# First stage of a decoder layer: x loaded by chunks, weight tiles contiguous, constants multiplied before x is there, seven PSUM banks, token rows loaded into the output buffer

## The chip, the cores and the metric

The kernel runs on one core of one Trainium2 chip. The metric is the device time of one execution in microseconds (us), the median of several runs. Beside it stands one profiled execution, from which every trace number comes. TensorE is called PE in the profile, its weight load PEld, VectorE DVE, ScalarE ACT, GpSimd POOL and SyncE SP; SP issues nearly all DMAs, in order.

## What is computed

One inference step of one decoder layer for 1024 prompt tokens and 8 x 4 sample tokens (1056 in all), model width 1024, in float32: a mixer (chunked gated MLP beside latent attention), cross-attention into a memory, and a gated convolution FFN. The change is in the first stage, the input projection:

```python
u, v, cq, ckv, kpe = split_in(rms_norm(xp, g_mix[l]) @ w_in[l])
a_out, _ = chunk_gmlp(u, v, w_s[l], b_s[l], ln_v_g[l], ln_v_b[l])
```

`chunk_gmlp` takes gelu(v), a layer norm over each group of 64 channels, multiplies each chunk of 128 tokens by a causal 128 x 128 matrix per group, adds a bias and multiplies by gelu(u). The same is done for the sample tokens.

## The kernel before, in words

**Split products.** A float32 operand is split into a high part (rounded to `FR`, float32r) and the rest, by `split` (L187): ScalarE makes the high part (L191, or L195 with the gain g_mix as scale), VectorE the low part (L192, L198). A product is three matmuls, high x high, high x low, low x high (`mm3`, L185).

**Order.** The framework orders the instructions of each engine when the kernel is built, by the order in which they are written and by its own simulated time; once built, the order of each engine is fixed. Between L337 and L428 a manual schedule keeps SP's DMAs in the written order.

**x twice.** The projection needs x with the 1024 channels on the partitions (input `xT`, 8 slices k of 128 channels), in three chunks of 384, 384 and 288 tokens (`CH`). Each chunk is loaded in two halves of four slices into `xr` (L317) and split into `xh`, `xl` (L353). The scale of rms_norm, one number per token, is applied after the projection; it needs x with tokens on the partitions (input `x`, nine token tiles `TILES` of 128, the last of 32). `squares` (L324) sums the squares of a tile on ScalarE (L332) and takes the inverse root on VectorE by a chain of eleven small instructions (`rsqrt`, L210 to L236); the result stands in `rs_tok`. Token tiles 0 to 2 go to buffers `xt` beside `xr` (L343 to L347). The pool of `xt` and `xr` is closed before `a_all`, the buffer of the stage's output, is opened in the same place (L365 to L367), and token tiles 3 to 8 are loaded into `a_all` while it is still unused (L371, L426).

**Weights.** The projection's columns come in six pieces: v0, v1, u0, u1 (256 columns each, u1 with the 32 of kpe) and a0, a1. `wraw` loads one in two halves into a buffer of [128, 8, 288], two such buffers in turn; of the 288 columns only the first n are used, so one row of a DMA is n elements. `wsplit` splits it.

**The loop** (L411) runs over two halves `hf`. In each, `proj` (L358) makes the v product of a token tile, 24 matmuls of 256 columns, into one of five PSUM banks with the tag "mm" (three more have the tag "st"); gelu with the scale rs_tok empties the bank on ScalarE (L435). Layer norm follows by groups of tiles (0 to 2, 3 to 5, 6 and 7, 8) on VectorE (L436 to L446), and on GpSimd with the gain and bias that `rows` brings (L448, L450, L453). After the first group of the first half, `gate_matrices` (L379) loads w_s, makes it causal on GpSimd (L383), splits it and prepares the sample tokens' version. Then come the nine u products (L464, gelu into `a_all` at L465), and the products of the gate matrices with the normed v (L474, L480). The rest of the stage makes the latents from a0 and a1 (L516 on). Later stages read `xT` once more as the residual (`out_proj`).

Of the kernel before, what the change touches and what calls it, by code (L numbers as in the profile page):

```python
# [5 lines left out]
F32 = mybir.dt.float32  # L6
FR = mybir.dt.float32r
I32 = mybir.dt.int32
AF = mybir.ActivationFunctionType
# [4 lines left out]
P = 128  # L14
NP_, NS, NT = 1024, 32, 1056
# [6 lines left out]
CH = [(0, 384), (384, 384), (768, 288)]  # L22
# [132 lines left out]
class Net:  # L155
# [132 lines left out]
    def phase1(self):  # L288
        nc, tc, I, O = self.nc, self.tc, self.I, self.O
        p = self.open("p1")  # L290
# [3 lines left out]
        pr = self.open("p1r", side="right")  # L294
        raws = {}

        def wraw(name, src, n):
            raws[name] = raw = self.t(pr, [P, 8, 288], F32, "wraw", 2)[:, :, :n]
# [13 lines left out]
        xts, xrs = [], []  # L312

        def xload(c, e):
            o, n = CH[c]
            xrs.append(self.t(px, [P, 4, 384], F32, "xr", 6)[:, :, :n])
            nc.sync.dma_start(xrs[-1], I["xT"][:, 4 * e : 4 * e + 4, o : o + n])  # L317

        def tload(i, place):
            t0, tn = TILES[i]  # L320
            xts.append(place[:tn])
            nc.sync.dma_start(xts[-1], I["x"][t0 : t0 + tn])

        def squares(p, i0, i1):  # L324

            ss = self.t(p, [P, 4], F32, "ss", 2)[:, : i1 - i0]
            if i1 == 9:
                nc.vector.memset(ss, 1.0)
            for i in range(i0, i1):
                xt = xts[i]  # L330
                tn = xt.shape[0]
                nc.scalar.activation(xt, xt, AF.Square, accum_out=ss[:tn, i - i0 : i - i0 + 1])  # L332
            self.rsqrt(p, self.rs_tok[:, i0:i1], ss, 1.0 / 1024)

        xt = lambda: self.t(px, [P, 1024], F32, "xt", 3)
        loads = tc.manual_schedule(engines={mybir.EngineType.SP})
        loads.__enter__()  # L337
        raws["v0"] = raw = self.t(pr, [P, 8, 288], F32, "wraw", 2)[:, :, :256]
# [4 lines left out]
        tload(0, xt())  # L343
        for e in range(2):
            xload(1, e)
        tload(1, xt())
        tload(2, xt())  # L347
        for e in range(2):
            xload(2, e)
# [8 lines left out]
        def proj(w, i, n):  # L358
            t0, tn = TILES[i]
            ps = self.t(pp, [P, 512], F32, "mm", 5)[:tn, :n]  # L360
# [5 lines left out]
        pl = self.open("pl")  # L366
        a_all = self.t(pl, [P, 9, 512], F32, "a_all")  # L367

        flat = a_all.rearrange("p i n -> p (i n)")
        for i in range(3, 7):  # L370
            tload(i, flat[:, (i - 3) * 1024 : (i - 2) * 1024])  # L371
# [4 lines left out]
        lng, lnb = rows[:, :512], rows[:, 512:]  # L376
        gates = {}

        def gate_matrices():  # L379

            ws = self.t(pg, [P, 8, P], F32, "ws")
            nc.sync.dma_start(ws, I["w_s"])
            nc.gpsimd.affine_select(ws, ws, [[0, 8], [1, P]], ALU.is_ge, 0.0, base=0, channel_multiplier=-1)  # L383
# [3 lines left out]
            sel = self.t(pg, [P, NS], F32, "sel")  # L387
            nc.sync.dma_start(sel, I["c_sel"])
            blk = self.t(pg, [NS, NS], F32, "blk")
            nc.sync.dma_start(blk, I["c_blk"])  # L390
            wsc = self.t(pg, [P, 8, ND], F32, "wsc")
            nc.gpsimd.tensor_copy(wsc, ws[:, :, :ND])
            st = self.t(pp, [P, 512], F32, "st", 3)
            nc.tensor.matmul(st[:NS, :32], sel, wsc.rearrange("p g t -> p (g t)"), start=True, stop=True)
# [12 lines left out]


        wraw("v1", I["w_v1"], 256)
        nc.sync.dma_start(self.ident, I["c_ident"])  # L410
        for hf in range(2):  # L411
            c0 = hf * 256
            nu = 288 if hf else 256
# [5 lines left out]
            vgs = self.t(pg, [NS, 256], F32, "vgs")  # L419
            for i0, i1 in ((0, 3), (3, 6), (6, 8), (8, 9)):  # L420
                m, tn = i1 - i0, TILES[i0][1]
                if hf == 0 and i0 in (3, 6):
                    squares(pg, i0, i0 + 3)
                if hf == 0 and i0 == 3:
                    for i in range(7, 9):
                        tload(i, flat[:, (i - 7) * 1024 : (i - 6) * 1024])  # L426
                    wraw("u1", I["w_u1"], 288)
                    loads.__exit__(None, None, None)  # L428
                gv = self.t(pg, [P, 3, 4, 64], F32, "gv", 2)[:tn, :m]
                mu = self.t(pg, [P, 3, 4], F32, "mu", 2)[:tn, :m]  # L430
                rv = self.t(pg, [P, 3, 4], F32, "rv", 2)[:tn, :m]
                for i in range(i0, i1):
                    ps = proj(w, i, 256)
                    g, mi = gv[:, i - i0], mu[:, i - i0]
                    nc.scalar.activation(g.rearrange("p g d -> p (g d)"), ps, AF.Gelu_apprx_tanh, scale=self.rs_tok[:tn, i : i + 1])  # L435
                    nc.vector.tensor_reduce(mi, g, AX.X, ALU.add)  # L436
                    nc.vector.tensor_scalar(mi, mi, 1.0 / 64, None, ALU.mult)
                    nc.vector.tensor_tensor(g, g, mi.unsqueeze(2).broadcast_to([tn, 4, 64]), ALU.subtract)
                    sq = self.t(pg, [P, 4, 64], F32, "gsq", 2)[:tn]
                    nc.scalar.activation(sq, g, AF.Square)  # L440
                    nc.vector.tensor_reduce(rv[:, i - i0], sq, AX.X, ALU.add)
                rf = rv.rearrange("p m g -> p (m g)")
                self.rsqrt(pg, rf, rf, 1.0 / 64)
                for i in range(i0, i1):
# [7 lines left out]
                    else:  # L452
                        nc.gpsimd.tensor_tensor(vgs, gf, lnb[:tn, c0 : c0 + 256], ALU.add)  # L453
                        nc.sync.dma_start(O["o_vg"][:, c0 : c0 + 256], vgs)
                if hf == 0 and i0 == 0:
                    gate_matrices()
                    wsh, wsl, bs_s, wss = (gates[x] for x in ("wsh", "wsl", "bs_s", "wss"))
            if hf == 0:
                w = wsplit("v1")
                wraw("a0", I["w_a"][0], 256)  # L460
            else:
                w = wsplit("a0")
            for i, (t0, tn) in enumerate(TILES):
                ps = proj(wu, i, nu)  # L464
                nc.scalar.activation(a_all[:tn, i, c0 : c0 + 256], ps[:, :256], AF.Gelu_apprx_tanh, scale=self.rs_tok[:tn, i : i + 1])  # L465
# [1101 lines left out]
    def out_proj(self, pp, p, mxs, ws, xh, xl, r3, end):  # L1567
# [741 lines left out]
```

## Time and profile before

| | us |
|---|---|
| median of 3 runs (lowest, highest) | 1870.41 (1868.35, 1872.27) |
| the profiled execution's own time | 1873.17 |
| its span, first to last instruction | 1871.5 |
| TensorE busy in the span | 1812.4 |
| VectorE, ScalarE, GpSimd busy | 1382.2, 928.9, 708.0 |
| mean granted TensorE clock | 0.991 |

A row of the order in time reads: start, duration, engine, line, operation, out<-in, shape, count, and in brackets the engine's idle time before it and what ended that. A wait row reads: who waited for whom, us in total, times, longest. A busy TensorE is not one at its peak, since matmuls overlap.

### The profile page before, as it was taken

The numbers are of one execution on the slowest core, as the hardware profiler recorded it, in microseconds if no ns is written. First come the engines' busy times: TensorE is split into PE (matmuls) and PEld (weight loads), VectorE is DVE, ScalarE is ACT, GpSimd is POOL, SyncE is SP. The second block draws the span as 40 slices with busy tenths as digits, with TensorE's granted clock in tenths as the row PEclk, the third lists the DMA queues.
The fourth block names the chain that finished last, engine by engine and source line by source line (L and its number), as shares of the span: only waits on it lengthen the run. The fifth ranks groups of instructions, "written<-read, shape, count | busy, mean of one in ns | idle before, by whom it ended". The sixth has DMA issues, their size and how long they took to land.

```text
span 1871.5 us, 39806 instructions
## 1 busy us (share of the span) xinstructions
PE 1812.4 (97%) x14402; PEld 1746.4 (93%) x14402; DVE 1382.2 (74%) x2883; ACT 928.9 (50%) x1965; POOL 708.0 (38%) x826
## 2 busy tenths in 40 slices
PE   6999899989999999999999999999999999999999
PEld 6999799889999999998799988899999999999999
DVE  6865967766887667776744676888888888878664
ACT  6435676666555655555533455633333333344442
POOL 1221515643535454443313110267776677500000
PEclk9999899999999999999999999999999999999999
DMA  8202204666776667564554345422222222495242
GB/s 286 70 10 68 82 1 165 222 230 175 219 205 186 180 173 200 162 186 128 182 157 134 135 158 154 129 67 81 81 82 90 69 72 77 113 352 167 78 154 76
DMA packets 139784, 260.18 MB, mean 139 GB/s; under 512 B 20546, under 2 KB 82851, under 8 KB 136515
## 3 DMA queue, kind: packets, MB, share of 16 engines
q1 hardware_dynamic: 138722, 256.58, 43.8%
q8 instruction: 114, 1.87, 0.4%
q10 hardware_dynamic: 864, 1.05, 0.2%
q14 instruction: 84, 0.68, 0.1%
HBM read 212.27 MB, written 45.30 MB: 138 GB/s over the span
## 4 chain that ended last, share of the span: by engine, by line
PE 61%; issue 5%; SPq 3%; DMA 3%; DVE 3%; POOL 2%; ACT 1%; POOLq 0%; DVEq 0%; ACTq 0%
PE d L185 12%; PE s L185 11%; PE b L185 7%; PE F L185 7%; PE X L185 6%; PE E L185 6%; PE A L185 3%; PE y L185 3%; DMA cT<-cT 2%; SPq L1220 2%; SPq L1224 1%; PE o L1367 1%; PE t L185 1%; POOL cl L1252 1%; PE v L185 1%
## 5 line engine op out<-in xcount | busy, mean ns | idle before, releaser
L185 PE MATMUL s<-w2h,ch 128*128 128x288 f32 (+1 forms) x1024 | 303.7, 297 | 0.0
L185 PE MATMUL s<-w2h,cl 128*128 128x288 f32 (+1 forms) x1024 | 296.0, 289 | 4.2 <-POOL cl L1252 3.0
L185 PE MATMUL s<-w2l,ch 128*128 128x288 f32 (+1 forms) x1024 | 294.6, 288 | 0.0
L185 PEld LDWEIGHTS s<-w2h,ch 128*128 128x128 f32 x1024 | 192.6, 188 | 8.3 <-ACT sq L1292 2.5
L185 PEld LDWEIGHTS s<-w2h,cl 128*128 128x128 f32 x1024 | 192.4, 188 | 6.5 <-POOL cl L1252 5.0
L185 PEld LDWEIGHTS s<-w2l,ch 128*128 128x128 f32 x1024 | 192.8, 188 | 0.0
L1295 DVE TENSOR_REDUCE ss<-sq 128x16 f32<-128x1024 f32 x128 | 155.3, 1213 | 32.4 <-ACT sq L1292 32.2
L1252 POOL TENSOR_TENSOR cl<-cT,ch 128x512 fp32r<-128x512 f32 x64 | 83.7, 1307 | 113.2 <-ACT ch L1248 92.5
L1292 ACT ACTIVATE sq<-s 128x512 f32<-128x512 f32 x128 | 76.6, 598 | 88.8 <-PE s L185 88.7
L1289 ACT ACTIVATE sq<-s 128x512 f32<-128x512 f32 x128 | 76.7, 600 | 74.5 <-PE s L185 74.0
L191 ACT CAST a<-brb 128x528 fp32r<-128x528 f32 x77 | 48.8, 634 | 111.4 <-PE d L185 107.9
L185 PE MATMUL mm<-whi,xh 128*128 128x256 f32 (+3 forms) x288 | 83.4, 291 | 16.4 <-ACT xh L195 10.0
L192 DVE TENSOR_TENSOR a<-brb,a 128x528 fp32r<-128x528 f32 x77 | 54.3, 707 | 58.3 <-ACT a L191 58.3
L185 PE MATMUL d<-a,w 128*128 128x264 f32 x768 | 95.4, 284 | 0.5 <-DVE G L2087 0.5
L185 PEld LDWEIGHTS d<-a,w 128*128 128x128 f32 x768 | 94.3, 188 | 0.7 <-issue 0.7
L932 PEld LDWEIGHTS o<-v,pth 128*128 128x128 f32 x576 | 75.7, 197 | 8.4 <-ACT pth L922 4.2
L185 PE MATMUL mm<-wlo,xh 128*128 128x256 f32 (+3 forms) x288 | 82.1, 288 | 0.0
L185 PE MATMUL mm<-whi,xl 128*128 128x256 f32 (+3 forms) x288 | 82.1, 289 | 0.0
L932 PE MATMUL o<-v,pth 128*128 128x64 f32 x576 | 76.3, 274 | 5.6 <-ACT pth L922 3.3
L1958 POOL TENSOR_TENSOR lo<-s,hi 128x1024 fp32r<-128x1024 f32 x20 | 62.9, 3142 | 45.7 <-ACT hi L1957 45.7
L1248 ACT CAST ch<-cT 128x512 fp32r<-128x512 f32 x128 | 73.4, 625 | 3.7 <-DMA cT<-cT 3.6
L2013 ACT COPY a<-A 128x264 f32<-128x264 f32 x43 | 16.1, 375 | 118.7 <-PE A L185 113.9
(725 smaller groups left out, 6447.5 us busy)
## 6 DMA issues: line engine op xcount, KB each, us to landing
cT<-cT SPq DMA_DIRECT2D x256, 160.0 KB, 2.8
ck<-ck SPq DMA_DIRECT2D x256, 144.0 KB, 3.4
raw<-w_up SPq DMA_DIRECT2D x44, 512.0 KB, 3.6
wsumd<-wsum SPq DMA_DIRECT2D x13, 1024.0 KB, 4.2
actd<-cv SPq DMA_DIRECT2D x44, 264.0 KB, 2.4
brb<-actd SPq DMA_DIRECT2D x44, 264.0 KB, 5.6
wsum<-w_down SPq DMA_DIRECT2D x11, 1024.0 KB, 5.0
raw<-wsumd SPq DMA_DIRECT2D x20, 512.0 KB, 3.7
```

Source lines behind the costliest of these rows:

```text
L185: self.nc.tensor.matmul(out, l, r, start=first and i == 0, stop=last and i == len(seq) - 1)
L191: {"act": nc.scalar.copy, "pool": nc.gpsimd.tensor_copy, "dve": nc.vector.tensor_copy}[eng](hi, src)
L192: low = lambda: nc.vector.tensor_tensor(lo, src, hi, ALU.subtract)
L932: nc.tensor.matmul(u["o"][:, e], th[:, z * P : z * P + P], s["v"][:, jj, h % 4], start=j == z == 0, stop=e == 1 and jj == 2 * G + 1)
L1220: dmas.append([nc.sync.dma_start(cT[:, j], I["cT"][bass.ds(rv, 1)].rearrange("a p n -> (a p) n")) for j, rv in enumerate(rvs)])
L1224: nc.sync.dma_start(ck[j * 32 : j * 32 + 32], I["ck"][bass.ds(rv, 1)].rearrange("a t s f -> (a t) s f"))
L1248: nc.scalar.copy(d["h"][:, k], src[k])
L1252: (nc.vector if k else nc.gpsimd).tensor_tensor(d["l"][:, k], src[k], d["h"][:, k], ALU.subtract)
L1289: nc.scalar.activation(sq[:, 0], ps[:, :, n0 : n0 + 256], AF.Square)
L1292: nc.scalar.activation(sq[:, 1], pt.rearrange("p (e d) -> p e d", e=2), AF.Square)
L1295: yield lambda: nc.vector.tensor_reduce(s["ss"][:, g0 : g0 + 2].rearrange("p e (z h) -> p z e h", z=2), sq.rearrange("p z e (h d) -> p z e ...
L1958: eng.tensor_tensor(lo, src, hi, ALU.subtract)
```

## The change

`xT` is stored chunk after chunk, so that a half chunk is one contiguous row of up to 1536 elements per partition, and `xr` has the same shape; a weight tile takes the first 8n elements of its buffer without gaps. `a_all` is opened before `xr`, in a place of its own, and every token tile is loaded into it: tile i takes the quarter i % 4, so tiles 4 to 8 wait until the square of the tile four before is done. `squares` takes three tiles at a time. `busy` multiplies a tile of ones (and then the first arrived pieces of w_v0 and xT) on TensorE into a bank that nobody reads, before the first product of x. The v0 products of the first six tiles are written ahead of the loop, the sixth and the seventh of them in "st" banks, and the remaining ones and two u0 products before the gelus of their groups. The loads of w_s and two small constants go into the manual order behind `rows`, and `gate_matrices` is called after all four groups of the first half instead of after the first.

```diff
-    o["xT"] = f(x.T.reshape(8, P, NT).transpose(1, 0, 2))
+    xT = x.T.reshape(8, P, NT).transpose(1, 0, 2)
+    o["xT"] = f(np.concatenate([xT[:, :, c : c + n].reshape(P, 8 * n) for c, n in CH], 1))
...
+        def wtile(n):
+            return self.t(pr, [P, 8, 288], F32, "wraw", 2).rearrange("p k n -> p (k n)")[:, : 8 * n].rearrange("p (k n) -> p k n", k=8)
...
+        pl = self.open("pl")
+        a_all = self.t(pl, [P, 9, 512], F32, "a_all")
         px = self.open("px")
...
+        st0 = self.t(pp, [P, 512], F32, "st", 3)
+        warm = self.t(px, [P, 512], F32, "warm")
+        nc.vector.memset(warm, 1.0)
+        def busy(x, n):
+            for _ in range(n):
+                nc.tensor.matmul(st0[:, : x.shape[1]], warm[:, :P], x, start=True, stop=True)
...
+        def tload(i):
             t0, tn = TILES[i]
+            xts.append(flat[:tn, i % 4 * 1024 : i % 4 * 1024 + 1024])
+            nc.sync.dma_start(xts[i], I["x"][t0 : t0 + tn])
...
+        busy(warm, 4)
+        raws["v0"] = raw = wtile(256)
         for e in range(2):
             k = slice(4 * e, 4 * e + 4)
             nc.sync.dma_start(raw[:, k], I["w_v0"][:, k])
             xload(0, e)
+            if e == 0:
+                busy(raw[:, :2].rearrange("p k n -> p (k n)"), 1)
+                busy(xrs[0][:, 0, :256], 1)
+        for i in range(3):
+            if i:
+                for e in range(2):
+                    xload(i, e)
+            tload(i)
         w = wsplit("v0")
         for c, (o, n) in enumerate(CH):
             for k in range(8):
                 self.split(xh[:, k, o : o + n], xl[:, k, o : o + n], xrs[2 * c + k // 4][:, k % 4], self.col("g_mix", k))
-            if c == 0:
-                squares(px, 0, 1)
-            elif c == 1:
-                squares(px, 1, 3)
+            if c == 1:
+                squares(0)
...
         self.close("px")
+        for i in range(3, 6):
+            tload(i)
         wraw("u0", I["w_u0"], 256)
+        tload(6)
+        squares(1)
+        for i in range(7, 9):
+            tload(i)
+        wraw("v1", I["w_v1"], 256)
         pg = self.open("pg")
...
+        ready = {i: proj(w, i, 256, ("mm", 5) if i < 5 else ("st", 3)) for i in range(6)}
+        us = {}
...
                 if hf == 0 and i0 == 3:
-                    for i in range(7, 9):
-                        tload(i, flat[:, (i - 7) * 1024 : (i - 6) * 1024])
+                    squares(2)
+                    ready[6] = proj(w, 6, 256, ("st", 3))
+                    ready[7] = proj(w, 7, 256)
                     wraw("u1", I["w_u1"], 288)
                     loads.__exit__(None, None, None)
+                elif hf == 0 and i0 == 6:
+                    ready[8] = proj(w, 8, 256)
+                    for i in range(2):
+                        us[i] = proj(wu, i, 256)
...
-                if hf == 0 and i0 == 0:
-                    gate_matrices()
-                    wsh, wsl, bs_s, wss = (gates[x] for x in ("wsh", "wsl", "bs_s", "wss"))
             if hf == 0:
+                gate_matrices()
+                wsh, wsl, bs_s, wss = (gates[x] for x in ("wsh", "wsl", "bs_s", "wss"))
                 w = wsplit("v1")
...
-            nc.sync.dma_start(res, I["xT"][:, m, o : o + n])
+            nc.sync.dma_start(res, I["xT"][:, 8 * o + m * n : 8 * o + m * n + n])
```

More of the change, by code (lines that the diff above doesn't have):

```diff
@@ L295, in phase1 @@
         raws = {}
+        def wtile(n):
+            return self.t(pr, [P, 8, 288], F32, "wraw", 2).rearrange("p k n -> p (k n)")[:, : 8 * n].rearrange("p (k n) -> p k n", k=8)
         def wraw(name, src, n):
-            raws[name] = raw = self.t(pr, [P, 8, 288], F32, "wraw", 2)[:, :, :n]
+            raws[name] = raw = wtile(n)
             for k in range(0, 8, 4):
@@ L324, in squares @@
-        def squares(p, i0, i1):
-            ss = self.t(p, [P, 4], F32, "ss", 2)[:, : i1 - i0]
-            if i1 == 9:
-                nc.vector.memset(ss, 1.0)
[L329 to L335, printed above, removed]
+            xrs.append(self.t(px, [P, 4, 384], F32, "xr", 6).rearrange("p k n -> p (k n)")[:, : 4 * n].rearrange("p (k n) -> p k n", k=4))
@@ L336, in phase1, with squares @@
+        def squares(c):
+            ss = self.t(pl, [P, 3], F32, "ss", 3)
+            if c == 2:
+                nc.vector.memset(ss, 1.0)
+            for i in range(3):
+                xt = xts[3 * c + i]
+                nc.scalar.activation(xt, xt, AF.Square, accum_out=ss[: xt.shape[0], i : i + 1])
+            self.rsqrt(pl, self.rs_tok[:, 3 * c : 3 * c + 3], ss, 1.0 / 1024)
         loads = tc.manual_schedule(engines={mybir.EngineType.SP})
         loads.__enter__()
-        raws["v0"] = raw = self.t(pr, [P, 8, 288], F32, "wraw", 2)[:, :, :256]
+        busy(warm, 4)
@@ L342, in phase1 @@
             xload(0, e)
[L343 to L349, printed above, removed]
+            if e == 0:
+                busy(raw[:, :2].rearrange("p k n -> p (k n)"), 1)
+                busy(xrs[0][:, 0, :256], 1)
+        for i in range(3):
+            if i:
+                for e in range(2):
+                    xload(i, e)
+            tload(i)
         w = wsplit("v0")
@@ L365, in phase1 @@
         self.close("px")
[L366 to L371, printed above, removed]
-        wraw("u0", I["w_u0"], 256)
+        for i in range(3, 6):
+            tload(i)
+        wraw("u0", I["w_u0"], 256)
+        tload(6)
[3 more added lines that the diff above has]
+        wraw("v1", I["w_v1"], 256)
         pg = self.open("pg")
@@ L376, in phase1 @@
         lng, lnb = rows[:, :512], rows[:, 512:]
+        ws = self.t(pg, [P, 8, P], F32, "ws")
+        nc.sync.dma_start(ws, I["w_s"])
+        sel = self.t(pg, [P, NS], F32, "sel")
+        nc.sync.dma_start(sel, I["c_sel"])
+        blk = self.t(pg, [NS, NS], F32, "blk")
+        nc.sync.dma_start(blk, I["c_blk"])
         gates = {}
         def gate_matrices():
-            ws = self.t(pg, [P, 8, P], F32, "ws")
-            nc.sync.dma_start(ws, I["w_s"])
             nc.gpsimd.affine_select(ws, ws, [[0, 8], [1, P]], ALU.is_ge, 0.0, base=0, channel_multiplier=-1)
```

26 lines of the change are left out of this document (9 added, 17 removed).

## The prediction

> **What bounds the kernel now.** I read the table of engines first, then the waits of the first 72 us, then TensorE (PE) and the engines that feed it in order of time, and last a table by stretches (in its rows, after the stretch: its length; busy us and instructions of PE, PEld, DVE, ACT, POOL; granted clock, DMA share, GB/s).
>
> ```profile
> PE 1812.4 (97%) x14402; PEld 1746.4 (93%) x14402; DVE 1382.2 (74%) x2883; ACT 928.9 (50%) x1965; POOL 708.0 (38%) x826
> ...
> PE mm L185 <- ACT xh L195: 10.0, 1, 10.0
> ...
> PE mm L185 <- ACT gv L435: 6.2, 2, 4.2
> ...
> SPq L322 <- DMA xr<-xT: 11.6, 1, 11.6
> ...
> 57.00:125.00 68.00, 68.00 (x545) 66.73 (x545) 51.23 (x158) 24.11 (x54) 22.07 (x27) 1.00 0.07 20
> ```
>
> TensorE is busy 97% of the span and without a break from 57 to 125 us, so what this stage can win is what TensorE loses before 57. The waits name it: 10.0 us until the first split x, and 6.2 us in two stops that ended when ScalarE's gelu (gv, L435) emptied a PSUM bank. VectorE has 16.8 us free in those 68, so work that it owes there can be paid later. The stops, and two stretches at half clock:
>
> ```profile
> 9.97 0.58 PE L185 MATMUL mm<-whi,xh 128*128 128x256 f32 x1 [9.97 <-ACT xh L195]
> ...
> 12.48 0.41 PE L185 MATMUL mm<-wlo,xh 128*128 128x256 f32 x1
> 12.70 0.33 PE L185 MATMUL mm<-whi,xl 128*128 128x256 f32 x1
> ...
> 12.98 0.28 PE L185 MATMUL mm<-wlo,xh 128*128 128x256 f32 x1
> 13.10 0.28 PE L185 MATMUL mm<-whi,xl 128*128 128x256 f32 x1
> ...
> 27.66 0.39 PE L185 MATMUL mm<-whi,xh 128*128 128x256 f32 x1 [1.96 <-ACT gv L435]
> 40.70 0.42 PE L185 MATMUL mm<-whi,xh 128*32 128x256 f32 x1 [4.21 <-ACT gv L435]
> 51.35 0.38 PE L185 MATMUL mm<-whi,xh 128*128 128x256 f32 x1 [0.29 <-ACT a_all L465]
> ```
>
> Up to 12.70 one matmul starts 0.21 us after the other, then 0.12. So from 9.97 to about 12.8 the array ran at half rate: 2.8 us that full rate does in 1.55, a loss of 1.25. The stop of 4.21 us brought this back, and here the granted clock (the third number from the right) shows it:
>
> ```profile
> 41.00:42.00 1.00, 1.00 (x7) 0.79 (x6) 1.00 (x4) 0.37 (x2) 1.00 (x2) 0.50 1.09 351
> ...
> 43.00:44.00 1.00, 1.00 (x9) 0.84 (x8) 1.00 (x3) 0.34 (x1) 1.00 (x2) 0.74 1.03 384
> ```
>
> From 40.7 to 43.5 again 2.8 us, again 1.25 lost. TensorE's losses before 57 are thus 9.97 + 1.25 + 1.96 + 4.21 + 1.25 + 0.29. Why the banks were late is in the feeding engines (SPq is the DMA queue on SP):
>
> ```profile
> 27.91 1.76 SPq L322 DMA_DIRECT2D a_all<-x  x4
> ...
> 26.00:27.00 1.00, 0.00 (x0) 0.00 (x0) 0.99 (x4) 1.00 (x3) 0.00 (x0) 1.00 0.00 0
> ...
> 25.44 1.81 ACT L195 ACTIVATE xh<-xr,cols 128x288 fp32r<-128x288 f32 x4 [1.17 <-DMA xr<-xT]
> 27.16 0.45 ACT L435 ACTIVATE gv<-mm,rs_tok 128x256 f32<-128x256 f32 x1
> ...
> 35.93 1.06 ACT L332 ACTIVATE a_all<-a_all 128x1024 f32<-128x1024 f32 x1 [0.19 <-DMA a_all<-x]
> 38.58 1.22 DVE L192 TENSOR_TENSOR wlo<-wraw,whi 128x1024 fp32r<-128x1024 f32 x1 [0.16 <-ACT whi L191]
> 38.94 1.04 ACT L191 CAST whi<-wraw 128x1024 fp32r<-128x1024 f32 x1 [0.40 <-DMA wraw<-w_u]
> 40.17 1.21 ACT L435 ACTIVATE gv<-mm,rs_tok 128x256 f32<-128x256 f32 x3 [0.18 <-DVE rs_tok L236]
> ```
>
> Token tiles 3 to 6 of x are issued only at 27.91, because their place overlaps the buffers of xT; the DMAs stand still (0 GB/s at 26:27). So the last square of tiles 3 to 5 starts at 35.93, their scale rs_tok is there at 40.1, and only then can gelu empty banks. The first stop is gelu of tile 0, held in ScalarE's order behind the last piece of xT (25.44).
>
> **The change part by part.**
>
> *Token x into a_all from the start.* This takes the 11.6 us wait out of SP's queue. Ahead of tiles 3 to 5 stand 7.0 MB (cols 0.07, w_v0 1.05, xT 4.33, three token tiles 1.57), which at some 380 GB/s from 3 us (rows of the start, below) end at 21.5; the next 1.57 MB need 4 us and land at about 26, nearly 10 us before 35.9; w_u0 follows at about 29. It adds waits: tiles 4 to 8 reuse places, so their loads, and u0, v1, rows and w_s behind them on SP, wait for squares on ScalarE. The first squares come behind chunk 1's split, about 18 us, before SP's DMAs run dry. I take nothing; a square that comes late holds these loads back, and costs at most the second stop and its cold stretch over again.
>
> *Seven banks.* The first seven tiles of v0 need no gelu; two more tiles are 2 x 24 matmuls x 0.12 = 5.7 us of work, more than the first stop. The scale of tiles 0 to 2 now needs all three token tiles, landing at some 21 to 22; with three squares and one root about 26.5. TensorE, starting at 8.6, has filled seven banks at 8.6 + 7 x 2.86 = 28.6. So 1.96 goes. After nine tiles (34.3) it needs w_u0, landed at 29, split with 2 x 1.04 on ScalarE and 2 x 1.22 on VectorE, and banks of tiles 3 to 5, whose scale I put at 31 to 33. So 4.21, its half clock of 1.25 and the 0.29 go; each release now comes only 1 to 3 us before it is needed, a thin cover that VectorE's load can use up (below).
>
> *The start.* Three terms meet: landing, split, warming.
>
> ```profile
> 6.58 1.04 ACT L191 CAST whi<-wraw 128x1024 fp32r<-128x1024 f32 x1 [4.28 <-DMA wraw<-w_v]
> 9.31 2.13 ACT L195 ACTIVATE xh<-xr,cols 128x384 fp32r<-128x384 f32 x4 [1.68 <-DMA xr<-xT]
> ...
> 3.00:4.00 1.00, 0.00 (x0) 0.00 (x0) 0.00 (x0) 0.00 (x0) 0.00 (x0) 1.00 1.00 210
> 4.00:5.00 1.00, 0.00 (x0) 0.00 (x0) 0.00 (x0) 0.00 (x0) 0.00 (x0) 1.00 0.92 234
> ...
> 6.00:7.00 1.00, 0.00 (x0) 0.00 (x0) 0.00 (x0) 0.42 (x1) 0.00 (x0) 1.00 1.03 364
> 7.00:8.00 1.00, 0.00 (x0) 0.00 (x0) 0.34 (x1) 0.63 (x1) 0.00 (x0) 1.00 1.07 387
> ...
> 31.00:32.00 1.00, 1.00 (x11) 1.00 (x10) 0.00 (x0) 0.28 (x1) 0.00 (x0) 1.00 1.07 426
> ```
>
> At 3:5 the queue carries w_v0 in rows of 1 KB and moves 210 to 234 GB/s with the DMA engines 92 to 100% busy; at 31:32 it carries rows of 4 KB and moves 426. Contiguous tiles make the first rows 4 and 6 KB. At 400 GB/s from 3.0 us the remaining 1.2 MB up to the first half of chunk 0 are through at 6.0, and land 1 to 1.9 later (the slowest engine): 7.0 to 7.9 in place of 9.2. The split adds 0.6: 7.6 to 8.5.
>
> Warming stands before it on TensorE: four products of 512 plain f32 columns, one more on w_v0, one of 256 on x. The trace has none that wide. The nearest rows:
>
> ```profile
> 50.45 0.25 PE L394 MATMUL st<-wsc,sel 128*32 128x32 f32 x2
> 1093.67 0.60 PE L1679 MATMUL t<-ident,pr 128*128 128x128 f32 x4
> ...
> 9.96 2.21 DVE L198 SCALAR_TENSOR_TENSOR xl<-xr,cols,xh 128x384 fp32r<-128x384 f32 x4 [1.07 <-ACT xh L195]
> ```
>
> One call is two instructions (L394), and 128 columns follow each other by (0.60 - 0.27) / 3 = 0.11 us; so 512 columns cost 2 x 0.44 = 0.87 us, 1.75 at half clock. The memset of 512 columns is not in the trace; one on 384 takes 0.55 (xl: four in 2.21), so TensorE can begin at about 1.4. With 2.8 us at half clock, as in both stretches above, the four end at 6.3, the fifth at 7.2, the sixth at 7.6 or when x lands. All at half clock they would end at 1.4 + 7.0 + 1.75 + 0.87 = 11.0. I take the first product at 8.6, near the short end because both measured stretches are short: a gain of 1.4, with ends of +2.4 and -1.0. The warming also covers the cold 1.25, which goes. The Trainium skill ("TensorE: Matmul & The Clock Gate", Part 1) has the gate look at free-running windows of about 3.4 us, so a burst may see almost two before it is freed; the traced 2.8 fits one. By two windows the first product would be near 9.5 and the sum 0.9 smaller.
>
> *The rest.* The gate matrices come later, and one of four root chains on VectorE goes (11 instructions of 0.16 = 1.8 us). Neither is on TensorE's path while VectorE keeps up. Loads of xT in the output stage keep their rows: 0.
>
> **Sum:** 1.4 + 1.25 + 1.96 + 4.21 + 1.25 + 0.29 = 10.4 us. The profiled execution took 1873.17 us (span 1871.5), so 1862.8 of its kind; the median of the runs shown, 1870.41, is 2.8 lower, and the forecast against it is **1860.0**.
>
> **Rivals.**
>
> *The first x lands no earlier.* The low rate at 3:5 can be the queue's start, not its rows: at 6:8 rows of 1 and 1.5 KB run at 364 to 387. Then the first product stays at 9.97, and only 9.0 is won: **1861.4**. The Trainium skill speaks for it: "DMA: Bandwidth & Descriptors" (Specifications) has full rate from 512 B on, so rows of 1 KB would lose nothing; the traced 210 beside 426 speaks against.
>
> *VectorE becomes the bound.*
>
> ```profile
> 7.50:57.00 49.50, 40.57 (x316) 39.17 (x317) 42.38 (x133) 34.75 (x68) 10.21 (x12) 0.97 0.81 285
> 33.21 0.74 DVE L441 TENSOR_REDUCE rv<-gsq 128x4 f32<-128x256 f32 x2 [2.35 <-ACT gsq L440]
> 42.14 1.10 DVE L437 TENSOR_SCALAR mu<-mu 128x4 f32<-128x4 f32 x3
> ```
>
> It has 42.4 us of work between 7.5 and 57, 40.6 without the root chain; with TensorE 10.4 earlier the stretch, from about 6.0 to 46.6, is 40.6 long: full. Idle such as the 2.35 behind ScalarE's gsq, and operations stretched beside GpSimd (three of 0.16 in 1.10), leave no room. For it to cost nothing, what is late must be layer norm, which TensorE needs only after u0, not rs_tok or the low weight parts. If some 5 us of such idle stay in front of these, VectorE is through at 51.6, and 5.4 is won: **1865.0**.
>
> *Gate matrices too late (slower).* They now stand behind all layer norms of the first half on GpSimd.
>
> ```profile
> POOL gv L448 <- DMA rows<-rows: 39.6, 1, 39.6
> ...
> 45.88 1.29 POOL L383 TENSOR_SCALAR_AFFINE_SELECT ws<-ws 128x1024 f32<-128x1024 f32 x1
> 47.23 1.08 POOL L392 COPY wsc<-ws 128x32 f32<-128x32 f32 x1
> ...
> 70.29 0.80 POOL L453 TENSOR_TENSOR vgs<-gv,rows 32x256 f32<-32x256 f32 x1
> ```
>
> If layer norm still ends at 71.1, then select 1.29, copy 1.08, and wsh and wsl, as long as whi and wlo (1.04, 1.22), follow: 75.7. TensorE is done with u0 at about 61. If its order puts the gate products ahead of v1, it waits 14.7 us and pays 1.25 of cold clock: 16 lost, 5.6 more than won: **1876**. It decides against the change once those matrices are over 10.4 us behind u0. Against it: the load of rows, for which GpSimd waited until 40.6 (39.6 from its last instruction on), lands some 5 us earlier.
>
> **How the numbers follow.** Forecast 0.50, late first x 0.15, VectorE 0.22, gate matrices 0.13. The forecast's own range is 1857 to 1864 (the start's ends, and 2 us either way as in the runs shown). The whole range, **1855 to 1868**, adds the second and third case and leaves out the last. 0.2% is 3.7 us, about what a measurement of this kernel can tell from no change. Faster: 0.48 + 0.15 + two thirds of 0.22 = 0.78; the same: 0.09; slower: 0.13.
>
> **What would show it.** TensorE's f32 products from about 1.4 us, its first split product at 7.6 to 9.5 with matmuls 0.12 apart at once; no stop over 1 us before 50; no half clock at 40 to 44; DMAs without a hole at 22 to 28; rs_tok of tiles 3 to 5 before 34; u0's last product near 60. A stop ended by rs_tok or wlo says VectorE, one ended by wsl the gate matrices. I am wrong if stops of over 4 us appear, or if the 10 us are there at 125 and gone at the end.

## The result, and the profile after

| | before | after |
|---|---|---|
| median, 22 runs each (us) | 1872.07 | 1867.72 |
| ratio, 95% interval | | 0.9982 [0.9974, 0.999] |
| the profiled execution's own time, span (us) | 1873.17, 1871.5 | 1868.82, 1867.1 |

The change wins 4.35 us by the medians of this comparison (3.4 by the ratio), where 10.4 were forecast. A second comparison, told below, gave 0.5 us with an interval that includes no change, so the size of the win is known only roughly.

The table of engines of the kernel after:

```profile
PE 1822.4 (98%) x14414; PEld 1754.4 (94%) x14414; DVE 1376.8 (74%) x2873; ACT 927.6 (50%) x1965; POOL 712.1 (38%) x826
```

TensorE is 10 us busier than before although the run is shorter: the products of `busy` count as work, some 7 us by the first three rows below. The busy share doesn't tell what was won; the order in time does. TensorE of the kernel after, in order of time:

```profile
1.53 5.28 PE L332 MATMUL st<-warm 128*128 128x512 f32 x8 [1.53 <-DVE warm L327]
6.64 1.02 PE L332 MATMUL st<-wraw,warm 128*128 128x512 f32 x2
7.91 0.70 PE L332 MATMUL st<-xr,warm 128*128 128x256 f32 x2 [0.25 <-DMA xr<-xT]
8.63 0.39 PE L185 MATMUL mm<-whi,xh 128*128 128x256 f32 x1
8.85 0.28 PE L185 MATMUL mm<-wlo,xh 128*128 128x256 f32 x1
8.97 0.29 PE L185 MATMUL mm<-whi,xh 128*128 128x256 f32 x1
...
60.82 0.28 PE L185 MATMUL mm<-whi,xl 128*32 128x256 f32 x1
64.82 1.19 PE L185 MATMUL mm<-vgh,wsh 128*128 128x512 f32 x4 [3.73 <-ACT vgh L191]
...
66.43 0.42 PE L185 MATMUL mm<-wlo,xh 128*128 128x256 f32 x1
66.64 0.41 PE L185 MATMUL mm<-whi,xl 128*128 128x256 f32 x1
...
127.65 0.45 PE L185 MATMUL mm<-xh,whi 128*128 128x384 f32 x1
```

The reader is to see three things. The first split product is at 8.63, and its matmuls are 0.12 us apart from the second (8.85) on. From there no stop stands in the order until 60.82, the last product of u0. Then TensorE waits 3.73 us for vgh, the high part of the normed v, and from 66.2 on one matmul starts 0.21 us after the other: half rate. ScalarE of the same kernel, where the casts to vgh of tiles 6 and 7 end at 63.19 and 64.77:

```profile
62.80 0.39 ACT L191 CAST vgh<-gv 128x256 fp32r<-128x256 f32 x1
64.06 0.41 ACT L462 ACTIVATE gsq<-gv 32x256 f32<-32x256 f32 x1 [0.88 <-DVE gv L460]
64.38 0.39 ACT L191 CAST vgh<-gv 128x256 fp32r<-128x256 f32 x1
```

The same places in the kernel before (GpSimd's last step of the normed v of tiles 6 and 7, ScalarE's cast of tile 7, VectorE's low parts vgl, then TensorE):

```profile
66.45 1.44 POOL L450 TENSOR_TENSOR gv<-gv,rows 128x256 f32<-128x256 f32 x2
...
67.92 0.41 ACT L191 CAST vgh<-gv 128x256 fp32r<-128x256 f32 x1 [0.29 <-DVE rqh L235]
...
69.20 1.29 DVE L192 TENSOR_TENSOR vgl<-gv,vgh 128x256 fp32r<-128x256 f32 x2
```

```profile
71.06 0.39 PE L185 MATMUL mm<-vgh,wsh 128*128 128x512 f32 x1
71.29 0.39 PE L185 MATMUL mm<-vgl,wsh 128*128 128x512 f32 x1
...
132.23 0.45 PE L185 MATMUL mm<-xh,whi 128*128 128x384 f32 x1
```

There the first product of the gate matrices followed u0 at 71.06 without a wait; vgh was ready at 68.33. The kernel after ends u0 at 60.94 (0.12 behind 60.82), **10.1 us ahead**. At the first product of a0, a row that every kernel here has (132.23 and 127.65), **4.6 are left**: 5.5 were lost at the gate products. By stretches, after (length; PE, PEld, DVE, ACT, POOL; clock, DMA share, GB/s):

```profile
3.00:4.00 1.00, 1.00 (x2) 0.34 (x1) 0.00 (x0) 0.00 (x0) 0.00 (x0) 1.00 0.89 246
4.00:5.00 1.00, 1.00 (x3) 0.41 (x2) 0.00 (x0) 0.00 (x0) 0.00 (x0) 1.00 1.04 289
...
26.00:27.00 1.00, 1.00 (x11) 1.00 (x10) 0.69 (x5) 0.70 (x1) 0.00 (x0) 1.00 1.01 401
6.00:61.00 55.00, 54.51 (x442) 51.79 (x440) 48.64 (x145) 39.16 (x79) 15.73 (x16) 1.00 0.69 265
...
67.00:68.00 1.00, 1.00 (x7) 1.00 (x6) 1.00 (x3) 0.23 (x1) 0.00 (x0) 0.50 0.03 8
...
27.80:62.30 34.50, 33.08 (x280) 32.15 (x278) 33.42 (x108) 20.03 (x43) 17.03 (x18) 1.00 0.46 163
```

The hole in the DMAs at 26:27 is gone (0 before, 401 GB/s now), TensorE is busy 54.5 of the 55 us from 6 to 61, the granted clock is 0.50 at 67:68, and VectorE is busy 33.42 of the 34.5 us in which most of the layer norm of the first half is made.

### The profile page after: what moved, and what is told of

It is laid out like the page before. It is cut to its first block, busy times and chain, and to the rows that moved or that the text cites. A ratio compares the mean times of both kernels' runs of the same rounds, so it can differ in the third digit from the quotient of the medians.

```text
span 1867.1 us, 39819 instructions
## 1 busy us (share of the span) xinstructions
PE 1822.4 (98%) x14414; PEld 1754.4 (94%) x14414; DVE 1376.8 (74%) x2873; ACT 927.6 (50%) x1965; POOL 712.1 (38%) x826
## 3 DMA queue, kind: packets, MB, share of 16 engines
q1 hardware_dynamic: 132578, 256.58, 44.1%
## 4 chain that ended last, share of the span: by engine, by line
PE 64%; issue 4%; DVE 3%; DMA 2%; POOL 2%; SPq 1%; ACT 1%; POOLq 0%; DVEq 0%; ACTq 0%
PE s L185 14%; PE d L185 12%; PE b L185 7%; PE X L185 7%; PE F L185 7%; PE E L185 7%; PE A L185 3%; PE y L185 3%; DMA cT<-cT 1%; PE o L1388 1%; SPq L1241 1%; PE t L185 1%; POOL cl L1273 1%; DMA ck<-ck 1%; DVE ss L1316 1%
## 5 line engine op out<-in xcount | busy, mean ns | idle before, releaser
L185 PE MATMUL mm<-whi,xh 128*128 128x256 f32 (+3 forms) x272 | 77.9, 288 | 0.0
L185 PE MATMUL mm<-wlo,xh 128*128 128x256 f32 (+3 forms) x272 | 77.7, 288 | 0.0
L185 PE MATMUL mm<-whi,xl 128*128 128x256 f32 (+3 forms) x272 | 77.3, 288 | 0.0
```

Source lines behind the costliest of these rows:

```text
L185: self.nc.tensor.matmul(out, l, r, start=first and i == 0, stop=last and i == len(seq) - 1)
```

## The experiments

**How they are read.** A median here moves by some 2 us between repetitions, and what lies behind the first product of a0 took 1735 to 1740 us in all the profiles, without order. So each experiment is read first at that row ("a0"), which repeats, and the median ratio to the kernel before stands beside it. "The wait" is TensorE's wait in front of the gate products. Three kernels ran twice for that; the first two:

> The kernel before, unchanged, against itself: how far two profiled executions of one kernel differ, and where. Theory (the first stage repeats, what spreads the times of one kernel by 5 us lies behind it): ratio 0.9985 to 1.0015, first product of a0 within 0.7 us of 132.23, rest of the span 1735 to 1740 us as in the other kernels' profiles. Rival (the first profile of the kernel before was a late one in its first stage, so the change's lead of 4.6 us at a0 is read too large): a0 at 129 to 131, which would make the lead 2 to 3 us, what the medians of two chips showed (4.4 and 0.5).

No edit. Ratio 0.9995 [0.9984, 1.0006]; a0 as in the first profile of before, within 0.3 us. TensorE of the second profile of before:

```profile
39.01 0.42 PE L185 MATMUL mm<-whi,xh 128*32 128x256 f32 x1 [4.40 <-ACT gv L435]
...
43.92 0.41 PE L185 MATMUL mm<-whi,xl 128*32 128x256 f32 x1
...
131.93 0.45 PE L185 MATMUL mm<-xh,whi 128*128 128x384 f32 x1
```

The theory holds at a0, but the way there differs: the first product was at 9.35 instead of 9.97, half rate from there lasted until 13.6 instead of 12.7, the stop of 1.96 us is not there, and the half rate behind the 4.40 lasted from 39.0 to 44.1 instead of 2.8 us. Terms of 1 to 2 us read from one execution are not all properties of the kernel.

> The kernel after, unchanged, as the base for the two kernels beside it. Theory (4.6 us of lead at the first product of a0, kept to the end): ratio to the kernel before 0.997 to 0.998, first product of a0 at about 127.7 us, TensorE waiting 3 to 4.5 us for the normed v before the gate products. Rival (what is won in the first stage is lost again later): ratio 0.999 to 1.001 with the same 127.7.

No edit. Ratio 0.9993 [0.9983, 1.0003] (1869.89 against 1870.41), a0 at 127.59, wait 3.65. The first stage repeats (a lead of 4.3 to 4.6 us over both profiles of before), the median's win does not: 4.35 us in one comparison, 0.5 in the other, which is the rival's ratio. Why part of the lead fails to arrive stays open; a difference of that size lies within the spread behind a0.

**Does the wait for the normed v take the 5.5 us?** Other work is put there:

```diff
+            if hf == 0:
+                for i in range(3):
+                    ready[i] = proj(w, i, 256)
             for g in range(4):
```

> The changed kernel with the v1 products of token tiles 0 to 2 written ahead of the first half's gate products. Theory (late layer norm): VectorE is full from 28 to 62 us, the normed v of tiles 6 and 7 comes at 64.8, and TensorE loses 3.7 us and then 1.7 us of half clock only because its order has the gate products next. With 8.6 us of v1 work in between, that stop and the half clock at 66 to 70 are gone, the first product of a0 (384 columns) starts at about 122.3 instead of 127.7, and the time is about 5.4 us under the changed kernel's: 1862, ratio 0.995. Rival (the stage is VectorE's as a whole): the stop turns up a few us later at another product, the first product of a0 stays at 126 to 128, ratio 0.997 to 0.999.

> The kernel after with three v1 products put between u0 and the gate products, a second time, beside the kernel after on the same chip. Theory (the whole 10.3 us of lead at a0 arrive): ratio to before 0.9945, about 5.7 us under the kernel after. Rival (part of the lead is lost in the attention and later): the first time's ratio of 0.9965 comes again, some 2 us under the kernel after. Both: a0 at 121.5 to 122.5, no wait for the normed v.

Ratios 0.9965 [0.9949, 0.998] and 0.9972 [0.996, 0.9984], medians 1863.95 and 1865.13. The first run, TensorE and a stretch:

```profile
69.50 0.40 PE L185 MATMUL mm<-vgh,wsh 128*128 128x512 f32 x1
...
121.95 0.45 PE L185 MATMUL mm<-xh,whi 128*128 128x384 f32 x1
```

```profile
6.00:188.00 182.00, 181.90 (x1362) 176.91 (x1360) 134.49 (x447) 97.06 (x236) 48.96 (x64) 1.00 0.31 110
```

The gate products now find their operands ready, TensorE has work for 181.9 of 182 us, the clock stays at 1.00, and a0 is at 121.95 (122.23 the second time): the whole 10 us are there. This shows that the wait and its half clock took the 5.5. Of 10.3 us at a0, 5 to 6 arrive in the medians, as far as these can tell. The second run doesn't decide between its theory and its rival: its ratio is near the rival's 0.9965, but against the kernel after on the same chip it is 4.8 us lower (5.4 at a0), near the theory's 5.7.

**Why does layer norm end so late?** First, more and less of VectorE's work (`more` is a product that nobody reads):

```diff
+                    if hf == 0 and i < 6:
+                        nc.vector.tensor_tensor(self.t(pg, [P, 4, 64], F32, "more"), g, g, ALU.mult)
```

> The changed kernel with one more VectorE operation of 128 x 256 (0.41 us; its result is not used) in the layer norm of each of token tiles 0 to 5 in the first half: 2.5 us of VectorE work. Theory (late layer norm, VectorE full): the normed v comes 2.5 us later and so does all behind it, the stop is about 6.2 us, the first product of a0 starts at about 130.2, ratio 0.9995. Rival (the layer norm is late by an order on ScalarE or by GpSimd, and VectorE has room): nothing moves by more than 0.5 us.

```diff
-                    nc.vector.tensor_scalar(mi, mi, 1.0 / 64, None, ALU.mult)
-                    nc.vector.tensor_tensor(g, g, mi.unsqueeze(2).broadcast_to([tn, 4, 64]), ALU.subtract)
+                    nc.vector.scalar_tensor_tensor(g, mi.unsqueeze(2).broadcast_to([tn, 4, 64]), -1.0 / 64, g, ALU.mult, ALU.add)
```

> The changed kernel with the layer norm's mean scaled and subtracted in one VectorE operation instead of two: nine operations less in the first half, 0.16 to 0.72 us each (0.31 on average). Theory (late layer norm, VectorE full): the normed v comes 1 to 2.5 us earlier, the stop is 1.2 to 2.7 us and too short for a half clock or just so, the first product of a0 starts at 124 to 126.5, ratio 0.996 to 0.9975. Rival (ScalarE's order or GpSimd sets the end of layer norm): it moves by less than 0.5 us.

With more work TensorE waits 6.34 us (ratio 0.9998 [0.9989, 1.0008], a0 130.73). ScalarE of that kernel shows that this isn't VectorE's amount alone:

```profile
64.48 0.39 ACT L191 CAST vgh<-gv 128x256 fp32r<-128x256 f32 x1
...
65.14 2.19 ACT L191 CAST whi<-wraw 128x1152 fp32r<-128x1152 f32 x2
67.23 0.40 ACT L191 CAST vgh<-gv 128x256 fp32r<-128x256 f32 x1
```

The cast of tile 6 ends 1.7 us later than in the kernel after (64.87 against 63.19), that of tile 7 2.9: GpSimd is through with tile 7 1.7 us later (64.65 against 62.97), and the order built for this kernel has two pieces of u1's weights (2.19) in between. With less work the wait is 3.05 us, a0 127.62, ratio 0.9986 [0.9975, 0.9998], so the theory's 124 to 126.5 is missed: the normed v of tile 7 ends no earlier (64.94 against 64.77). Its first product was at 9.77, over 1 us later, so one can say at most that about 1 us was made up.

Then the place of the work. VectorE and GpSimd of the kernel after, in front of the gate products:

```profile
54.90 0.70 DVE L233 TENSOR_TENSOR rqa<-rqy 128x8 f32<-128x8 f32 x1
55.64 0.66 DVE L234 TENSOR_TENSOR rqa<-rqa,rqx 128x8 f32<-128x8 f32 x1
...
57.73 0.66 DVE L231 SCALAR_TENSOR_TENSOR rqa<-rqy 128x8 f32<-128x8 f32 x1
58.42 0.17 DVE L234 TENSOR_TENSOR rqa<-rqa,rqx 128x8 f32<-128x8 f32 x1
...
58.82 0.17 DVE L236 SCALAR_TENSOR_TENSOR rv<-rqh,rqy 128x8 f32<-128x8 f32 x1
```

```profile
53.91 2.36 POOL L470 TENSOR_TENSOR gv<-gv,rows 128x256 f32<-128x256 f32 x3 [5.67 <-DVE gv L468]
56.23 2.13 POOL L472 TENSOR_TENSOR gv<-gv,rows 128x256 f32<-128x256 f32 x3
...
61.20 1.77 POOL L472 TENSOR_TENSOR gv<-gv,rows 128x256 f32<-128x256 f32 x2
```

Five instructions on 8 columns take 0.66 to 0.70 us each while GpSimd puts gain and bias on tiles 3 to 5, and 0.17 once it is done at 58.4; three of the five rows are shown. They belong to the inverse root of tiles 6 and 7, the last that the gate products wait for. The edit takes GpSimd's part away at the price of more work on VectorE:

```diff
-                    nc.gpsimd.tensor_tensor(gf, gf, lng[:tn, c0 : c0 + 256], ALU.mult)
+                    eng = nc.vector if hf == 0 and i0 == 3 else nc.gpsimd
+                    eng.tensor_tensor(gf, gf, lng[:tn, c0 : c0 + 256], ALU.mult)
...
-                        nc.gpsimd.tensor_tensor(gf, gf, lnb[:tn, c0 : c0 + 256], ALU.add)
+                        eng.tensor_tensor(gf, gf, lnb[:tn, c0 : c0 + 256], ALU.add)
```

> In the first half, gain and bias of the layer norm of tiles 3 to 5 (six GpSimd instructions of 0.70 us) are put on VectorE (six of 0.34 to 0.41). Theory (VectorE is held beside GpSimd: in the kernel after five small instructions of the inverse root of tiles 6 and 7 take 0.66 to 0.70 instead of 0.16 while GpSimd does this work, and three low parts 2.69 instead of 1.2, 4 us in all): VectorE has 2 to 2.5 us more to do and still ends earlier, the wait before the gate products is 1.7 to 2.5 us instead of 3.7, a0 at 125.5 to 126.7. Rival (the amount of VectorE's work sets the end): the wait grows to about 6 us, a0 at 129.5 to 130.5.

Wait 3.26, a0 126.83, ratio 0.9995 [0.9984, 1.0007]. VectorE and ScalarE of this kernel:

```profile
54.19 0.16 DVE L233 TENSOR_TENSOR rqa<-rqy 128x8 f32<-128x8 f32 x1
54.27 1.09 DVE L471 TENSOR_TENSOR gv<-gv,rows 128x256 f32<-128x256 f32 x3
...
55.35 1.09 DVE L473 TENSOR_TENSOR gv<-gv,rows 128x256 f32<-128x256 f32 x3
...
58.47 0.15 DVE L236 SCALAR_TENSOR_TENSOR rv<-rqh,rqy 128x8 f32<-128x8 f32 x1
```

```profile
61.49 2.19 ACT L191 CAST whi<-wraw 128x1152 fp32r<-128x1152 f32 x2
63.59 0.71 ACT L191 CAST vgh<-gv 128x256 fp32r<-128x256 f32 x2
```

The rival is refuted as it was put: 2.2 us more work on VectorE, and the wait doesn't grow. VectorE's busy time is another thing: from 27.8 to 62.3 us it was 32.95 here and 33.42 in the kernel after, since the stretching is gone and the small instructions are back at 0.16. The theory's 1.7 to 2.5 us of wait is missed too: the last instruction of the inverse root starts at 58.47 instead of 58.82, since the moved work stands in the same place, and on ScalarE two pieces of u1's weights (2.19 us) now precede the normed v of tiles 6 and 7. GpSimd was through with tile 7 at 62.24 instead of 62.97, so that part of the chain did get shorter, but the casts started only at 63.59.

The order on ScalarE was to be tested with tile 8, which the gate products don't need, and both edits together:

```diff
-            for i0, i1 in ((0, 3), (3, 6), (6, 8), (8, 9)):
+            def norm(i0, i1):
...
+            for i0, i1 in ((0, 3), (3, 6), (6, 8), (8, 9))[: 3 + hf]:
+                norm(i0, i1)
...
+            if hf == 0:
+                norm(8, 9)
             st = self.t(pp, [P, 512], F32, "st", 3)
```

> The layer norm of token tile 8 of the first half, which the gate products don't need, is written behind those products instead of ahead of u0. Theory (ScalarE's fixed order holds the normed v: gelu of tile 8 waits 3.25 us and the square of tile 8 stands ahead of the normed v of tile 7): normed v of tile 7 at about 63.3 instead of 64.8, wait 2.2 to 2.5 us, a0 at 125.9 to 126.3. Rival (GpSimd and VectorE set the end): wait 3.4 to 4, a0 at 127.3 to 128.

> The two edits beside it together: gain and bias of tiles 3 to 5 on VectorE, layer norm of tile 8 behind the gate products. Theory (two holds one behind the other): the wait before the gate products is at most 1 us, no half clock there, a0 at 123 to 125. Rival (VectorE's amount of work): a0 at 128.5 or later.

Waits 3.74 and 3.38, a0 128.50 and 127.35, ratios 0.9974 [0.9959, 0.9989] and 0.9979 [0.9962, 0.9996]. ScalarE of the first, which has tile 8 written later:

```profile
63.25 0.46 ACT L457 ACTIVATE gv<-mm,rs_tok 32x256 f32<-32x256 f32 x1 [3.26 <-DVE vgl L192]
63.62 0.39 ACT L191 CAST vgh<-gv 128x256 fp32r<-128x256 f32 x1
64.89 0.42 ACT L462 ACTIVATE gsq<-gv 32x256 f32<-32x256 f32 x1 [0.88 <-DVE gv L460]
65.21 0.39 ACT L191 CAST vgh<-gv 128x256 fp32r<-128x256 f32 x1
```

Tile 8's gelu and square stand where they stood before, in between the two normed v: the order that the framework built has them there again, so the edit didn't do what it says, and the pair decides nothing on ScalarE's order. It suggests something else: here the first product was at 9.46, 0.83 later than in the kernel after, and a0 is 0.85 later with the same wait, so a late start can move layer norm with it. The second run of the kernel after bears this out only in part: a first product 0.56 later, a gate product 0.20 later.

**The other parts of the change.** The ones products taken out (`busy`, `warm` and `st0` removed):

```diff
-        busy(warm, 4)
...
-                busy(raw[:, :2].rearrange("p k n -> p (k n)"), 1)
-                busy(xrs[0][:, 0, :256], 1)
```

> The changed kernel without the tile of ones and its products. Theory (late layer norm): the first products of x run 2.8 us at half clock, u0 ends 1.2 us later (62.3) and the stop at the gate products is 1.2 us shorter; the first product of a0 stays at 127 to 128, ratio 0.998. Rival (early work is carried through): it starts 1.2 us later or, if the ones held x back, as much earlier; ratio off by 0.0007 either way.

```profile
8.78 0.58 PE L185 MATMUL mm<-whi,xh 128*128 128x256 f32 x1 [8.78 <-ACT xh L195]
...
12.37 0.41 PE L185 MATMUL mm<-whi,xh 128*128 128x256 f32 x1
12.58 0.34 PE L185 MATMUL mm<-wlo,xh 128*128 128x256 f32 x1
...
66.68 0.50 PE L185 MATMUL mm<-vgh,wsh 128*128 128x512 f32 x1 [4.25 <-ACT vgh L191]
```

Ratio 1.0003 [0.9989, 1.0016], a0 129.51. TensorE runs at half rate until 12.7 again (0.21 apart), and the wait for vgh is 0.5 longer. a0 is 1.9 us later than in the kernel after: without the ones the cold stretch is back, and only 0.15 us of the difference stand in the time of the first product. The theory is missed: it had layer norm end at its own time and a0 stay at 127 to 128, and the loss is more than the rival's 1.2. GpSimd's last step for tile 7 ended 0.7 us later (63.65 against 62.97), and the cast behind it 1.9 later, with two pieces of u1's weights ahead of it on ScalarE. Layer norm's end moves with TensorE's start and with the order built.

The banks, in the kernel after and in the one with v1 first:

```diff
-        ready = {i: proj(w, i, 256, ("mm", 5) if i < 5 else ("st", 3)) for i in range(6)}
+        ready = {i: proj(w, i, 256) for i in range(6)}
...
-                    ready[6] = proj(w, 6, 256, ("st", 3))
+                    ready[6] = proj(w, 6, 256)
```

> The changed kernel with the v0 products in five banks instead of seven. Theory (late layer norm): TensorE stops about 4 us for a bank between 23 and 28 us, ends u0 at about 65 and then finds the normed v there; the wait only moves, the first product of a0 starts at 127 to 129, ratio 0.998. Rival (the seven banks are what the change won): it starts 4 to 6 us later, at 131.5 to 133, ratio 1.000 to 1.001.

> The changed kernel with v1 products ahead of the gate products and with five banks for v0. Theory (a lead is worth what the next late thing leaves of it): without the wait for the normed v nothing gives the lost banks back; a stop of about 4.3 us at 24 to 29 and up to 3.4 us of half-clock loss stay, and the first product of a0 starts at 126 to 129 (121.95 with seven banks), ratio 0.998 to 0.999. Rival (seven banks are worth nothing in either order): it starts at 122 to 123.5, ratio 0.9965.

The first of the two:

```profile
28.82 0.58 PE L185 MATMUL mm<-whi,xh 128*128 128x256 f32 x1 [4.29 <-ACT gv L457]
```

Both stop for a bank at 28 (4.29 and 4.49 us). Ratios 0.9986 [0.9975, 0.9998] and 0.9996 [0.9987, 1.0006], a0 130.05 and 128.47. With v1 first the two more banks are worth 6.5 us at a0 (128.47 against 121.95); in the kernel after only 2.4 (130.05 against 127.65), since there the stop for the bank gives layer norm the time that it needs: with five banks nothing waits for vgh. In mechanism this is the theory; in size the first of the two fell between theory and rival (its first product, at 9.76, was 1.1 us late), and the second is within its theory.

The gate matrices back behind the first group of tiles:

```diff
+                if hf == 0 and i0 == 0:
+                    gate_matrices()
+                    wsh, wsl, bs_s, wss = (gates[x] for x in ("wsh", "wsl", "bs_s", "wss"))
             if hf == 0:
-                gate_matrices()
-                wsh, wsl, bs_s, wss = (gates[x] for x in ("wsh", "wsl", "bs_s", "wss"))
```

> The changed kernel with the gate matrices called after the first group of the first half, as before. Theory (late layer norm): wsl was there at 48.2 and the stop was for the normed v, so nothing moves: a stop of 3 to 4.5 us ended by the normed v, the first product of a0 at 127 to 128.5, ratio 0.998. Rival (the move of the gate matrices cost it): the stop shrinks below 2 us and that product starts before 125.5, ratio 0.997.

```profile
69.79 1.05 PE L502 MATMUL st<-vgs,wss 32*32 32x64 f32 x8 [7.54 <-POOL vgs L475]
```

Ratio 1.0018 [1.0008, 1.0028], a0 132.92, the latest of all kernels; no theory had it slower. In the order built for it, the sample tokens' products (vgs, which GpSimd finishes last) stand in front of the gate products, and TensorE waits 7.54 us. The late gate matrices of the change were no loss; their old place, in the order built for it, would have been one.

The start alone, put into the kernel before (chunk-major xT, weight tiles in one piece, the ones products; nothing else of the change):

```diff
+    o["xT"] = f(np.concatenate([xT[:, :, c : c + n].reshape(P, 8 * n) for c, n in CH], 1))
...
+        busy(warm, 4)
```

> The kernel before with the new start alone: xT by chunks, weight tiles in one piece, ones multiplied; five banks, token rows loaded as before. Theory (TensorE's lead is worth what the next late thing leaves of it): the first product comes at 8.6 at full clock, a lead of 2.6 us, but the two stops for banks end when the scales are there, a little earlier than at 27.7 and 40.7; the first product of a0 (132.2 before) starts at 130.5 to 132, ratio 0.999 to 1.000. Rival (the start is worth its own length): it starts at 129.6, ratio 0.9986.

Ratio 0.9995 [0.9985, 1.0005], median 1868.15 against 1870.23, a0 130.54: 1.4 to 1.7 us ahead of the two profiles of before, as the theory had it, and not told from no change by the median.

**A version that beats both** has v1 first and the mean in one instruction:

> v1 products first as in the kernel beside it, and the mean of layer norm scaled and subtracted in one VectorE instruction in place of two. Theory (once TensorE has other work, layer norm of the first half isn't waited for, so less VectorE work there gives nothing): a0 at 121.5 to 122.5, time within 1 us of the kernel beside it. Rival (VectorE's load holds other things of the stage too): a0 1 us or more earlier, time 1 to 2 us lower.

Ratio 0.9958 [0.9944, 0.9971], median 1863.13 against 1870.41, a0 122.47, wait none. It is beyond both kernels; against the one with v1 first alone (0.9972 [0.996, 0.9984]) it can't be told apart, though its median is 2.0 us lower, and at a0 it isn't earlier, as the theory had it.

## Why the prediction was wrong, point by point

**The step that failed** is the sentence "Neither is on TensorE's path while VectorE keeps up", and behind it, in the rival on VectorE, that what is late costs nothing if it is layer norm, "which TensorE needs only after u0". The cover of that sentence was never worked out. It stood in the profile of before, in the rows above: vgh of tile 7 ended at 68.33 and was needed at 71.06, a cover of 2.7 us. With u0 done 10.1 us earlier, layer norm had to end 7.4 us earlier to be missed by nobody; it ended 3.6 earlier (64.77). The rest, 3.8, is the wait of 3.73. By the starts it is 3.9 (the next product at 64.82 instead of 60.94). With it came 3.4 us at half clock, in which some 16 matmuls start 0.21 us apart instead of 0.12: 1.5 lost, together 5.4 of the 10.1. That other work at this place brings it all back is shown by the two runs with v1 first.

**Why layer norm came only 3.6 us earlier** is shown in part. The rows of GpSimd and ScalarE split it. In the kernel before GpSimd was through with tile 7 at 67.89 and ScalarE cast it at 67.92. In the kernel after GpSimd was through at 62.97, 4.9 us earlier, but the cast started only at 64.38: in ScalarE's order the square of tile 8 stood ahead of it and waited for VectorE. So of the 3.8 us that were missing, some 1.4 were ScalarE's order and 2.5 lay ahead of it. This is read from the trace; no run tests it. Ahead of it VectorE was full (33.42 of 34.5 us), and the inverse root of tiles 6 and 7 was stretched beside GpSimd from 0.17 to 0.7 us an instruction. That the amount of work given to VectorE alone sets the end is refuted. The Trainium skill ("SBUF — State Buffer", Who interferes with whom) has a VectorE instruction with two inputs in SBUF contend with a GpSimd instruction that reads SBUF; the five of 0.66 to 0.70 us, each about as long as one of GpSimd's three in 2.13 to 2.36, agree. A VectorE instruction with one input (TENSOR_SCALAR on 4 columns, at 65.10 in the kernel before) was stretched beside GpSimd too, to 0.71 us; that sentence doesn't cover it. What the 2.5 us ahead of ScalarE are made of can't be settled: every edit of this stretch gave a new built order, with waits between 3.05 and 6.34 us and never none.

**The terms of the sum** came, all before 61 us, with 10.1 us of lead for 10.4 (9.6 between the second profiles of both kernels):

- *Start, 1.4:* 8.63 for a forecast of 8.6. But it is a term of one execution: the fourteen profiles with the ones products have their first product between 8.63 and 9.77, 9.2 in the mean, the two of before at 9.97 and 9.35. The gain is nearer 0.5, and that 8.6 was met is luck.
- *First x by rows:* the queue still moved only 246 and 289 GB/s at 3:5, with rows of 4 and 6 KB. Most of the low rate belongs to the queue's start, as the rival said, though the full case of that rival (9.97) didn't come in this profile, and two of the fourteen came near it (9.76 and 9.77).
- *First cold clock, 1.25:* it came; without the ones it is back, until 12.7.
- *Bank stops, 1.96 and 4.21, with the second cold clock and the 0.29:* all gone; with five banks a stop of 4.29 is back. The scale of tiles 0 to 2 was ready at 26.83 for a forecast of 26.5, that of tiles 3 to 5 at 35.02 instead of 31 to 33, and still in time.

**The rivals.** "VectorE becomes the bound" was nearest in size (5.4 won, against 4.35 measured and 4.6 at a0), by another place: it had rs_tok or the low weight parts late, and these weren't; that the sizes are near each other is chance. "Gate matrices too late" had the right place and the wrong operand: wsl was done at 48.18. The list of what would show an error had no row for vgh, the one that showed it. That the measured 1867.72 lies inside the whole range, 1855 to 1868, speaks for no step of the forecast: that end was added for the rivals.

## What to carry to other kernels

When a change lets the bounding engine run ahead, list every operand that it will need in the won time and write beside each how long it lay ready before the change: that slack, not the engine's busy share, is what the gain may use up. Here the row of vgh would have said that no more than 2.7 of 10 us were free without speeding up layer norm, and that of the low part vgl (through at 70.49, used at 71.29) only 0.8. TensorE didn't wait for vgl in the kernel after only because the order built for it put products of v1 between vgh and vgl. Where the feeding chain can't be made faster, put independent work of the bounding engine in front of the late operand.

## What the runs showed of the hardware

- The half-rate stretch behind a stop isn't of one length: 2.8 us in the first profile of before, 5.1 in the second (39.0 to 44.1) behind nearly the same stop (4.21 and 4.40). In the kernel after it began only 1.4 us after the restart (64.82, 66.2); in its second profile, behind a stop of 3.65, at the restart itself. The Trainium skill ("TensorE: Matmul & The Clock Gate", Part 1) has windows that run free of the kernel's own times; these rows agree.
- The first DMAs of the kernel after ran at 246 to 289 GB/s at 3:5 even in rows of 4 to 6 KB, and at 401 at 26:27.
- A VectorE instruction on 8 columns took 0.66 to 0.70 us beside GpSimd's work and 0.17 without it, so these five steps of the inverse root, each of which needs the one before it, took about four times as long there.
